# Scale of the first h summed on TensorE with its lower halves on VectorE, and the second layer's residual weighted beside the latent heads

## The chip, the cores and the metric

The kernel runs on one core of one Trainium2 chip. The metric is the device time of one launch in microseconds; of several runs the median is taken. The engines are named as in the profile: PE is TensorE (PEld its weight loads), DVE is VectorE, ACT is ScalarE, POOL is GpSimd, SP is SyncE, which here only issues DMAs.

## The reference

Two post-norm layers over x, 1024 tokens by 1024 features, batch 1, conditioned on one vector c:

```python
for l in range(DEPTH):
    mod = jax.nn.silu(c) @ w_ada[l] + b_ada[l]
    shift, scale, gate = jnp.split(mod, 3, axis=-1)
    h = x * (1.0 + scale[:, None, :]) + shift[:, None, :]
    (...) = jnp.split(h @ w_in[l], SPLIT_POINTS, axis=-1)
    ...  # o_a: 6 latent (MLA) heads, o_b: 6 dilated heads, o_c: 4 sparse heads with an indexer
    y = jnp.concatenate([o_a, o_b, o_c], axis=-1) * jax.nn.silu(p_gate)
    sub = y @ w_out[l]
    x = layer_norm(ALPHA * x + (1.0 + gate[:, None, :]) * sub, ln_g[l], ln_b[l])
```

Two things matter here. The first layer's `h` needs the scale and the shift, two products of a 1024-vector with a 1024x1024 matrix. And the second layer's residual is `ALPHA * x`, where x is the first layer's normalized output times `ln_g[0]` plus `ln_b[0]`.

## The kernel before, in words

**Precision.** A big fp32 product is made as three products of fp32r halves: an operand is split into a rounded upper half (`hi`, by ScalarE, AF.Copy) and a lower half (`lo = raw - hi`, by VectorE or GpSimd). `split_w` (L188) loads a weight tile into a raw buffer and makes both halves; its lower half is GpSimd's unless `lo_eng` says otherwise (L193).

**Order.** The program is written operation by operation; a scheduler with a timeline model (L1063) then sets the order of each engine's queue and inserts the waits, so the order of the code is a priority and not the order of execution. Each engine runs its own queue in order.

**The opening, `begin` (L883 to L946).** Eight steps, one for each block of 128 features. `part_ada(k)` loads two 128x1024 tiles of the modulation weights (e = 0 the scale, e = 1 the shift; w_ad0, L905). VectorE sums the tile's eight 128x128 pieces, weighted by the columns of silu(c) (`cs`): one operation at L913 and seven at L915. One fp32 matmul with a column of ones (L916) adds up the 128 partitions and leaves a column in the PSUM tile `o_ps` (O in the profile), and L918 adds the bias: `mod0`. `part_h(k)` loads x transposed (L922), in every other step a tile of the value weights `wvb` (L924, with a split), applies scale and shift on ScalarE (L927), rounds (L928), and makes the lower half at L929, on GpSimd but for the last step. `part_vb(k)` adds the step's 21 matmuls (three products for seven token blocks, L899) to seven PSUM banks. LEAD = 3 says how many steps `part_ada` is written ahead of `part_h`. The value blocks then leave PSUM (`values_b`), and the indexer follows (`indexer`, L387), whose first weights are split on GpSimd too, and beside which the other modulation vectors are summed on VectorE (`later`, `ada`, L256).

**The heads.** Each layer runs the dilated heads, the threshold search (`select`), the sparse heads and then the latent heads (`mla`, L679). In `attend` (L296) TensorE makes the scores of a block, VectorE takes the minimum on the way out of PSUM, ScalarE the exponential, GpSimd scales by the reciprocal of the sum (L293), TensorE transposes (L315), ScalarE and VectorE split (L318, L319), TensorE multiplies by the values (L327), and GpSimd applies the gate (L334). Other GpSimd work in `mla`: lower halves of keys (L721), of queries (L725) and of weights (L193).

**The end of a layer, `out_proj` (L792).** The gated y and the output weights are split (L800, L818). Then, for each block of 128 tokens in the order 7 to 0: the residual is loaded into a buffer of the ring XR (L841); two half rows of 24 matmuls each are multiplied by 1 + gate (L856), the residual is added (L857), statistics are taken (L858 to L863, with a power on GpSimd). In layer 1 the block is normalized and written to `x1_d` without ln_g and ln_b, which are folded into the next layer's scale and shift. In layer 2 the residual is therefore weighted first: GpSimd multiplies it by ln_g[0] (L843) and adds ln_b[0] (L844); the result is normalized with ln_g[1] and ln_b[1] at L867 and L868 and stored. XR has one buffer in layer 1 and two in layer 2. The four rows of ln_g and ln_b go to buffers that the heads have used (`lgb`, L824).

Of the kernel before, what the change touches and what calls it, by code (L numbers as in the profile page):

```python
# [13 lines left out]
OP = mybir.AluOpType  # L14
# [25 lines left out]

NLD = 8
NX = 6
LEAD = 3

NQ = ((2,2,3,4,6,6,6),(2,2,3,4,6,6,6))

# [14 lines left out]
KE = (1,1)  # L61

NPL = 2

EARLY = (2,2)
FB = ((0,2,4,0,2,0),(1,3,1,1,1,1))
# [40 lines left out]
def trunk(ctx: ExitStack, tc: tile.TileContext, a, out):  # L107
# [31 lines left out]
    scr, scr8 = [scrf[:, i * 256:i * 256 + 256].bitcast(mybir.dt.uint8) for i in range(2)]  # L139
    o_ps = ps_o.tile([P, 2, 256], F32, name="O")  # L140

    ident = sb.tile([P, P], F32, name="ident")
    causb = sb.tile([P, 512], BF16, name="causb")
    dist2 = sb.tile([P, 2 * P], BF16, name="dist2")
# [35 lines left out]
    kr_d = dr.tile([32, 1024], F32, name="kr_d")  # L180
    g1_d = [dr.tile([1, 1024], F32, name=f"g1_d{i}") for i in range(DEPTH)]
    x1_d = [dr.tile([P, 1024], F32, name=f"x1_d{i}") for i in range(NB)]


    def bc(t):
# [493 lines left out]
    def mla(l, values):  # L679
# [77 lines left out]

            project(wh, wl, 6, CA, evac)

        q, y = {}, {}  # L760
        keys(0)
        key(0)
        query(0)
# [4 lines left out]
        for h in range(6):  # L768
            if h % 2 == 0:
                y[h // 2] = G.next()  # L770
                sp.dma_start(y[h // 2], ga_d[h // 2])
            Kh, Kl = KA[h % 2]
            Qh, Ql = q[h]

            def done(g, yt=y[h // 2], yo=HA[h // 2], c=None):
                c = c or slice(g * 256, g * 256 + 256)
                act.activation(yo[0][:, c], yt[:, c], AF.Copy)
                pool.tensor_tensor(yo[1][:, c], yt[:, c], bc(yo[0][:, c]), OP.subtract)

            attend(f'A{h}', [(Qh, Kh), (Ql, Kh), (Qh, Kl)], vblk((h + 4) % 6), None, scq, y[h // 2],  # L780
                   (h % 2) * 64, ORDA[l], done if h in (3, 5) else None, PACK[l] and slots(h))
            if h < 4:
                if h % 2 == 0:
                    keys(h // 2 + 1)
                    if h == 2:
                        done(0, y[0], HA[0], slice(0, 1024))
                key(h + 2)
            for i in range(NQ[l][h], NQ[l][h + 1]):
                if i < 5:
                    query(i)  # L790

    def out_proj(l):  # L792
        last = l == DEPTH - 1
        order = [3, 4, 5, 6, 7, 0, 1, 2]
        Y = HA
        for k in order[:5]:
            raw = WR.next()
            sp.dma_start(raw, y_d[k])
            act.activation(Y[k][0], raw, AF.Copy)
            (pool if k in YP[l] else dve).tensor_tensor(Y[k][1], raw, bc(Y[k][0]), OP.subtract)  # L800


        Vs = [VS[0][:, i * 1024:(i + 1) * 1024] for i in range(6)]
        f = G.n % 2 ^ 1
        XR = Ring([AC[0]] + ([G.tiles[f]] if last else []))
        at = {3: (Vs[4], Vs[5]), 4: (Vs[0], Vs[1]), 5: W.tiles[0:2], 6: W.tiles[2:4],
              7: (fresh(f"g{1 - f}", F32R), fresh("bi1", F32R)), 0: held[0:2], 1: held[2:4],
              2: (Vs[2], [fresh(f"rw{n}", F32R, 512) for n in range(2)])}
        wo = {}
        for k in order:  # L810
            raw = WR.next()
            sp.dma_start(raw, a["w_out"][l, k])
            hi, lo = at[k]
            eng = pool if k in WP[l] else dve
            for n in range(2):
                c = slice(n * 512, n * 512 + 512)
                act.activation(hi[:, c], raw[:, c], AF.Copy)
                eng.tensor_tensor(lo[n] if k == 2 else lo[:, c], raw[:, c], bc(hi[:, c]), OP.subtract)  # L818
            wo[k] = [(hi[:, n * 512:n * 512 + 512], lo[n] if k == 2 else lo[:, n * 512:n * 512 + 512]) for n in range(2)]
        g1 = BI.tiles[0]  # L820
        sp.dma_start(g1, g1_d[l].to_broadcast([P, 1024]))
        lgb = []
        if last:
            for t, src in zip([fresh("pt0", F32), fresh("pt1", F32), PR3[2], PR3[1]],  # L824
                              (a["ln_g"][0], a["ln_b"][0], a["ln_g"][1], a["ln_b"][1])):
                sp.dma_start(t, src.to_broadcast([P, 1024]))
                lgb.append(t)
        else:

            lnc = small.tile([P, 2, 8], F32, name="lnc", bufs=1)  # L830
            sp.dma_start(lnc, a["ln_c"])
            dve.tensor_tensor(lnc[:, 0, :], lnc[:, 0, :], scale1_n, OP.mult)
            dve.tensor_tensor(lnc[:, 1, :], lnc[:, 1, :], scale1_n, OP.mult)
            dve.tensor_tensor(lnc[:, 1, :], lnc[:, 1, :], shift_n, OP.add)
        X = Ring(AC[1:4] + [PR3[0]])
        PR.tiles = [G.tiles[f]]
        xs = {}
        for tb in TBO:
            tok = slice(tb * P, (tb + 1) * P)
            xr = XR.next()  # L840
            sp.dma_start(xr, x1_d[tb] if last else a["x"][tb])  # L841
            if last:
                pool.tensor_tensor(xr, xr, lgb[0], OP.mult)  # L843
                pool.tensor_tensor(xr, xr, lgb[1], OP.add)  # L844
            r = X.next()
            st = small.tile([P, 2, 6], F32, name="st")
            for n in range(2):
                cols = slice(n * 512, n * 512 + 512)
                ps = (ps_p if n else ps_s).tile([P, 512], F32, name="pj" if n else "S")
                items = []  # L850
                for k in order:
                    yh, yl = Y[k]
                    w0, w1 = wo[k][n]
                    items += [(yh[:, tok], w0), (yl[:, tok], w0), (yh[:, tok], w1)]
                chain(ps, items)
                dve.tensor_tensor(r[:, cols], ps, g1[:, cols], OP.mult)  # L856
                dve.scalar_tensor_tensor(r[:, cols], xr[:, cols], ALPHA, r[:, cols], OP.mult, OP.add)  # L857
                dve.bn_stats(st[:, n, :], r[:, cols])  # L858
            mv = small.tile([P, 2], F32, name="mv")
            dve.bn_aggr(mv, st)  # L860
            rs = small.tile([P, 1], F32, name="rs")
            dve.tensor_scalar(rs, mv[:, 1:2], 1e-5, None, OP.add)  # L862
            pool.tensor_tensor(rs, rs, mhalf, OP.pow)  # L863
            if last:
                for n in range(2):
                    cols = slice(n * 512, (n + 1) * 512)
                    dve.scalar_tensor_tensor(r[:, cols], r[:, cols], mv[:, 0:1], lgb[2][:, cols], OP.subtract, OP.mult)  # L867
                    dve.scalar_tensor_tensor(r[:, cols], r[:, cols], rs, lgb[3][:, cols], OP.mult, OP.add)  # L868
                    sp.dma_start(out[tb][:, cols], r[:, cols])
                continue  # L870
            dve.tensor_scalar(r, r, mv[:, 0:1], rs, OP.subtract, OP.mult)
            sp.dma_start(x1_d[tb], r)
            xs[tb] = r
            if len(xs) == 4:
                for k in range(8):
                    t = ps_t.tile([P, 512], F32, name="T")
                    for j in range(4):
                        pe.transpose(t[:, j * P:(j + 1) * P], xs[tb // 4 * 4 + j][:, k * P:(k + 1) * P], ident)
                    mod_h(t, tb // 4, k, PR.next(), lnc[:, 0, :], lnc[:, 1, :])
                xs = {}  # L880


    def begin():  # L883
# [18 lines left out]
        def part_ada(k):  # L902
            for e in range(2):
                w = ring.next()
                sp.dma_start(w, a["w_ad0"][e, k])  # L905
                if k == 0 and e:
                    sp.dma_start(bcol, a["b_ad0"])
                    dve.tensor_scalar(bcol[:, 0, :], bcol[:, 0, :], 1.0, None, OP.add)
                part = cols[:, (2 * k + e) % 8, :]
                for c in range(8):  # L910
                    wc = w[:, c * P:(c + 1) * P]
                    if c == 0:
                        dve.tensor_scalar(part, wc, cs[:, 0:1], None, OP.mult)  # L913
                    else:
                        dve.scalar_tensor_tensor(part, wc, cs[:, c:c + 1], part, OP.mult, OP.add)  # L915
                pe.matmul(o_ps[:, 0, 2 * k + e:2 * k + e + 1], lhsT=part, rhs=ones, start=True, stop=True,  # L916
                          skip_group_check=True)
            dve.tensor_tensor(mod0[:, :, k], o_ps[:, 0, 2 * k:2 * k + 2], bcol[:, :, k], OP.add)  # L918

        def part_h(k):  # L920
            x = xs.next()
            sp.dma_start(x, a["xt"][k])  # L922
            if k % 2 == 0:
                hi, lo = split_w(a["wvb"][0, k // 2], 784, ring=QK, raws=raws)  # L924
                for j in range(2):
                    wv.append((hi[:, j * 392:(j + 1) * 392], lo[:, j * 392:(j + 1) * 392]))
            act.activation(x, x, AF.Identity, scale=mod0[:, 0, k:k + 1], bias=mod0[:, 1, k:k + 1])  # L927
            act.activation(HA[k][0], x, AF.Copy)  # L928
            (dve if k == 7 else pool).tensor_tensor(HA[k][1], x, bc(HA[k][0]), OP.subtract)  # L929

        for k in range(-LEAD, 9):
            if 0 <= k + LEAD < 8:
                part_ada(k + LEAD)
            if 0 <= k < 8:
                part_h(k)
            if k > 0:
                part_vb(k - 1)
        sp.dma_start(ident, a["ident"])
# [128 lines left out]
```

## Time and profile before

| | us |
|---|---|
| median of three runs | 1795.9 |
| the three runs | 1790.45 to 1797.68 |
| the profiled execution | 1791.37 |
| its span | 1789.5 |
| TensorE busy | 1662.4 |
| VectorE busy | 1396.6 |
| ScalarE busy | 1022.0 |
| GpSimd busy | 697.8 |

The span runs from the first instruction to the last; the remaining 1.9 us lie around it. A timeline row gives the start, the duration, the engine, the line, the operation, what it writes and reads, and how many were merged into the row; in brackets stands how long the engine was idle before it and what released it. In the rows of one line, three durations in ns are the shortest, the median and the longest. A row of the waits gives who waited for whom: us in total, times, and the longest. A row of the groups gives busy us, mean ns and the idle time before them.

### The profile page before, as it was taken

To read this page: it belongs to the slowest core of one execution; us is meant where nothing else is said; L and a number is where in the kernel's file an instruction comes from. 1 tells how busy PE (TensorE), PEld (TensorE's weight loads), DVE (VectorE), ACT (ScalarE), POOL (GpSimd) and SP (SyncE) were. 2 spreads that over 40 slices of the span, in tenths; PEclk is the share of its full clock that TensorE was granted. 3 is DMA by queue.
4 is the path that set the end of the run, shared out by engine and by line. 5 is a ranking of instruction groups with operands and counts; after the bars stand their busy time and mean duration, and the time that the engine had idled before them with its cause. 6 is when DMAs were issued, how large, how long until landed. Compare 5 with 4: busy or idle time off the path is not lost. (4 is left out here: it accounts for less than half of the span.)

```text
span 1789.5 us, 26735 instructions
## 1 busy us (share of the span) xinstructions
PE 1662.4 (93%) x9080; PEld 1440.0 (80%) x9080; DVE 1396.6 (78%) x3266; ACT 1022.0 (57%) x2010; POOL 697.8 (39%) x625
## 2 busy tenths in 40 slices
PE   4899899999998999989999989999999999998993
PEld 4778688888896888877899978888789788987882
DVE  8889788889588678886763678888948866788589
ACT  3244499895544666674113649998544367767500
POOL 3421134233434355463322113323343345666274
PEclk9899999999999999999999999999999999999997
DMA  9465113233212521222332212242220244122232
GB/s 345 147 220 189 48 55 92 78 119 102 75 36 62 212 92 57 84 68 92 110 130 51 71 59 56 75 142 83 74 92 20 67 171 141 45 76 91 71 106 94
DMA packets 55364, 178.93 MB, mean 100 GB/s; under 512 B 7606, under 2 KB 8630, under 8 KB 54716
## 3 DMA queue, kind: packets, MB, share of 16 engines
q1 hardware_dynamic: 50812, 147.86, 24.7%
q0 software_dynamic: 4416, 29.36, 5.7%
q8 instruction: 72, 1.18, 0.3%
q14 instruction: 64, 0.52, 0.1%
HBM read 129.74 MB, written 34.87 MB: 92 GB/s over the span
## 5 line engine op out<-in xcount | busy, mean ns | idle before, releaser
L199 PE MATMUL pj<-h,w 128*128 128x512 f32 (+1 forms) x3408 | 831.1, 391 | 13.9 <-DVE qk L233 5.4
L199 PEld LDWEIGHTS pj<-h,w 128*128 128x128 f32 x3408 | 632.2, 191 | 131.6 <-issue 12.6
L193 POOL TENSOR_TENSOR w<-wr,w 128x1024 fp32r<-128x1024 f32 (+2 forms) x86 | 192.9, 2244 | 284.4 <-ACT w L192 262.7
L199 PE MATMUL S<-qk,qk 128*128 128x512 f32 (+2 forms) x1104 | 281.9, 360 | 11.0 <-DVE mx L283 4.6
L293 POOL TENSOR_SCALAR pr<-pr,den 128x896 f32<-128x896 f32 (+7 forms) x180 | 139.0, 776 | 257.3 <-DVE den L292 214.0
L318 ACT ACTIVATE pt<-T 128x512 fp32r<-128x512 f32 (+1 forms) x320 | 172.1, 551 | 112.6 <-PE T L315 56.3
L319 DVE TENSOR_TENSOR pt<-T,pt 128x512 fp32r<-128x512 f32 (+1 forms) x320 | 199.6, 633 | 43.1 <-ACT pt L318 38.9
L327 PE MATMUL O<-pt,v 128*128 128x256 f32 (+1 forms) x1280 | 213.0, 286 | 7.3 <-DVE pt L319 4.2
L199 PEld LDWEIGHTS S<-qk,qk 128*128 128x128 f32 x1104 | 185.2, 191 | 36.7 <-DVE mx L283 8.7
L480 ACT ACTIVATE scr<-acc,U 128x768 uint8<-128x768 f32 x186 | 193.2, 1039 | 33.6 <-DVE U L476 18.1
L327 PEld LDWEIGHTS O<-pt,v 128*128 128x128 f32 x1280 | 185.6, 191 | 24.0 <-DVE pt L319 6.8
L334 POOL TENSOR_TENSOR g<-g,osum 64x256 f32<-64x256 f32 x128 | 98.6, 770 | 224.0 <-DVE osum L332 222.3
L291 ACT ACTIVATE pr<-pr,mx 128x384 f32<-128x384 f32 (+7 forms) x188 | 145.6, 775 | 54.7 <-DVE mx L283 36.4
L315 PE MATMUL T<-ident,pr 128*128 128x128 f32 x852 | 144.7, 278 | 9.7 <-POOL pr L293 5.1
L462 DVE TENSOR_SCALAR_CACHE_REDUCE scr<-acc,U 128x384 uint8<-128x384 f32 x186 | 138.4, 744 | 3.8
L192 ACT ACTIVATE w<-wr 128x1024 fp32r<-128x1024 f32 (+2 forms) x86 | 83.8, 976 | 65.0 <-PE pj L199 62.3
L315 PEld LDWEIGHTS T<-ident,pr 128*128 128x128 f32 x852 | 101.4, 141 | 21.0 <-POOL pr L293 6.5
L199 PE MATMUL pj<-w,h 128*128 128x256 f32 (+2 forms) x672 | 107.0, 300 | 1.4 <-DMA h<-cq_d 1.2
L199 PEld LDWEIGHTS pj<-w,h 128*128 128x128 f32 x672 | 91.7, 190 | 6.3 <-DMA h<-cq_d 1.4
L331 ACT ACTIVATE osum<-O 64x256 f32<-64x256 f32 x128 | 48.6, 380 | 58.5 <-PE O L327 55.3
L436 DVE SCALAR_TENSOR_TENSOR acc<-S,wi,acc 128x512 f32<-128x512 f32 (+1 forms) x84 | 56.2, 679 | 30.6 <-ACT S L431 30.3
L332 DVE TENSOR_TENSOR osum<-O,osum 64x256 f32<-64x256 f32 x128 | 53.4, 417 | 26.2 <-ACT osum L331 22.6
(277 smaller groups left out, 2565.2 us busy)
## 6 DMA issues: line engine op xcount, KB each, us to landing
wr<-in_wt_dram SPq DMA_DIRECT2D x62, 512.0 KB, 3.6
cq_d<-rw SPq DMA_DIRECT2D x64, 256.0 KB, 2.0
h<-cq_d POOLq DMA_DIRECT2D x4, 4096.0 KB, 20.2
qk<-qk POOLq DMA_DIRECT2D x48, 256.0 KB, 2.9
pt<-in_w_ada_dram SPq DMA_DIRECT2D x22, 512.0 KB, 4.0
wr<-in_w_out_dram SPq DMA_DIRECT2D x16, 512.0 KB, 3.5
bi<-in_bias_dram SPq DMA_DIRECT2D x14, 512.0 KB, 4.1
bi<-in_w_ada_dram SPq DMA_DIRECT2D x10, 512.0 KB, 4.5
```

The lines of the kernel that those rows point to most:

```text
L192: act.activation(hi[:, :n], raw[:, :n], AF.Copy)
L193: (lo_eng or pool).tensor_tensor(lo[:, :n], raw[:, :n], bc(hi[:, :n]), OP.subtract)
L199: pe.matmul(ps, lhsT=l, rhs=r, start=(i == 0), stop=(i == len(items) - 1))
L291: act.activation(p[:, :n], p[:, :n], AF.Exp, bias=m, scale=-1.0, accum_out=den)
L293: (dve if ne[qb] else pool).tensor_scalar(p[:, :n], p[:, :n], den, 0.5, OP.mult, OP.mult)
L315: pe.transpose(t[:, c:c + P], p[j](2 * kp + kk), ident)
L318: act.activation(pt[:, 0, :n], t[:, :n], AF.Copy)
L319: dve.tensor_tensor(pt[:, 1, :n], t[:, :n], bc(pt[:, 0, :n]), OP.subtract)
L327: pe.matmul(o[:, oc], lhsT=vt(kb), rhs=pt[:, e, pc], start=(kb == 0 and e == 0), stop=(kb == 2 * g + 1 and e == 1), skip_group_check=True)
L334: pool.tensor_tensor(yc, yc, s[r0:r0 + 64], OP.mult)
L462: dve.tensor_scalar(scr8[:, :IDX_LEN[b]], scores(b), s, None, op, OP.add, accum_out=dst[:, b:b + 1])
L480: act.activation(scr[:, :IDX_LEN[b]], scores(b), AF.Sign, bias=U[:, b:b + 1].bitcast(F32), accum_out=cnt[:, b:b + 1])
```

## The change

Three parts. First, in the opening, the scale half of the modulation (e = 0) is no longer summed on VectorE: eight fp32 matmuls per step take the 128x128 pieces of the raw weight tile as the stationary operand and a column of `cs` as the moving one, and accumulate in the same column of O. The shift half stays. The lower halves of h (L929) and of the value weights (`split_w` in `part_h`) go from GpSimd to VectorE. LEAD becomes 1, and `part_h(k)` is written ahead of `part_ada(k + 1)`.

Second, in layer 2 the weighted residual is made earlier: `residual(i)` loads a block of `x1_d` into a new tile RES, GpSimd multiplies by ln_g[0] and adds ln_b[0] (in the new tiles LNG and LNB), and the block is stored to `xw_d`. Two blocks are written after each of the heads 0 to 3 (NRES). `out_proj` of layer 2 loads `xw_d`; LNG and LNB then take ln_g[1] and ln_b[1].

Third, RES is a further buffer of the ring XR in both layers, so two in layer 1 and three in layer 2. The three new tiles take 12 KiB per partition; the scratch of the GpSimd-issued DMAs is set to 4096.

```diff
-LEAD = 3
+LEAD = 1
+NRES = ((0,0,0,0,0,0),(2,2,2,2,0,0))
...
+    RES, LNG, LNB = [sb.tile([P, 1024], F32, name=n) for n in ("res", "lng", "lnb")]
...
+    xw_d = [dr.tile([P, 1024], F32, name=f"xw_d{i}") for i in range(NB)]
...
-        q, y = {}, {}
+        q, y, rest = {}, {}, list(range(NB))
...
+            for _ in range(NRES[l][h]):
+                residual(rest.pop(0))
+
+    def residual(i):
+
+        if i == 0:
+            sp.dma_start(LNG, a["ln_g"][0].to_broadcast([P, 1024]))
+            sp.dma_start(LNB, a["ln_b"][0].to_broadcast([P, 1024]))
+        tb = TBO[i]
+        sp.dma_start(RES, x1_d[tb])
+        pool.tensor_tensor(RES, RES, LNG, OP.mult)
+        pool.tensor_tensor(RES, RES, LNB, OP.add)
+        sp.dma_start(xw_d[tb], RES)
...
-        XR = Ring([AC[0]] + ([G.tiles[f]] if last else []))
+        XR = Ring([AC[0], RES] + ([G.tiles[f]] if last else []))
...
-        lgb = []
         if last:
-            for t, src in zip([fresh("pt0", F32), fresh("pt1", F32), PR3[2], PR3[1]],
-                              (a["ln_g"][0], a["ln_b"][0], a["ln_g"][1], a["ln_b"][1])):
-                sp.dma_start(t, src.to_broadcast([P, 1024]))
-                lgb.append(t)
+            sp.dma_start(LNG, a["ln_g"][l].to_broadcast([P, 1024]))
+            sp.dma_start(LNB, a["ln_b"][l].to_broadcast([P, 1024]))
...
-            sp.dma_start(xr, x1_d[tb] if last else a["x"][tb])
-            if last:
-                pool.tensor_tensor(xr, xr, lgb[0], OP.mult)
-                pool.tensor_tensor(xr, xr, lgb[1], OP.add)
+            sp.dma_start(xr, xw_d[tb] if last else a["x"][tb])
...
-                    dve.scalar_tensor_tensor(r[:, cols], r[:, cols], mv[:, 0:1], lgb[2][:, cols], OP.subtract, OP.mult)
-                    dve.scalar_tensor_tensor(r[:, cols], r[:, cols], rs, lgb[3][:, cols], OP.mult, OP.add)
+                    dve.scalar_tensor_tensor(r[:, cols], r[:, cols], mv[:, 0:1], LNG[:, cols], OP.subtract, OP.mult)
+                    dve.scalar_tensor_tensor(r[:, cols], r[:, cols], rs, LNB[:, cols], OP.mult, OP.add)
...
-                part = cols[:, (2 * k + e) % 8, :]
+                to = o_ps[:, 0, 2 * k + e:2 * k + e + 1]
+                if e == 0:
+
+                    for c in range(8):
+                        pe.matmul(to, lhsT=w[:, c * P:(c + 1) * P], rhs=cs[:, c:c + 1], start=(c == 0), stop=(c == 7),
+                                  skip_group_check=True)
+                    continue
+
+                part = cols[:, k % 8, :]
...
-                hi, lo = split_w(a["wvb"][0, k // 2], 784, ring=QK, raws=raws)
+                hi, lo = split_w(a["wvb"][0, k // 2], 784, ring=QK, lo_eng=dve, raws=raws)
...
-            (dve if k == 7 else pool).tensor_tensor(HA[k][1], x, bc(HA[k][0]), OP.subtract)
+            dve.tensor_tensor(HA[k][1], x, bc(HA[k][0]), OP.subtract)
 
         for k in range(-LEAD, 9):
+            if 0 <= k < 8:
+                part_h(k)
             if 0 <= k + LEAD < 8:
                 part_ada(k + LEAD)
-            if 0 <= k < 8:
-                part_h(k)
...
-    nc = bacc.Bacc("TRN2", target_bir_lowering=False, num_devices=1)
+    nc = bacc.Bacc("TRN2", target_bir_lowering=False, num_devices=1, dynamic_dma_scratch_size=4096)
```

More of the change, by code (lines that the diff above doesn't have):

```diff
@@ L915, in part_ada @@
                         dve.scalar_tensor_tensor(part, wc, cs[:, c:c + 1], part, OP.mult, OP.add)
-                pe.matmul(o_ps[:, 0, 2 * k + e:2 * k + e + 1], lhsT=part, rhs=ones, start=True, stop=True,
-                          skip_group_check=True)
+                pe.matmul(to, lhsT=part, rhs=ones, start=True, stop=True, skip_group_check=True)
             dve.tensor_tensor(mod0[:, :, k], o_ps[:, 0, 2 * k:2 * k + 2], bcol[:, :, k], OP.add)
```

## The prediction

> **What bounds the kernel now.** I read the busy time by stretch of the span first, then the waits and the timeline of the two stretches in which TensorE is not busy.
>
> ```profile
> 0.00:74.30 74.30, 42.43 (x200) 39.45 (x200) 63.46 (x156) 25.48 (x28) 33.43 (x17) 0.93 0.71 255
> 74.30:1480.00 1405.70, 1352.07 (x7355) 1169.11 (x7356) 1091.79 (x2604) 848.35 (x1677) 488.15 (x455) 0.99 0.30 95
> 1480.00:1600.00 120.00, 119.22 (x744) 106.64 (x743) 91.09 (x245) 84.04 (x173) 72.47 (x73) 1.00 0.23 70
> 1600.00:1620.00 20.00, 14.45 (x86) 13.08 (x84) 16.22 (x34) 14.68 (x27) 16.72 (x11) 0.91 0.42 138
> 1620.00:1715.00 95.00, 90.92 (x510) 76.50 (x511) 63.46 (x144) 49.47 (x108) 45.10 (x51) 0.98 0.25 81
> 1715.00:1760.60 45.60, 43.34 (x190) 35.22 (x189) 45.46 (x50) 0.00 (x0) 32.94 (x15) 1.00 0.29 98
> 1760.60:1789.50 28.90, 0.00 (x1) 0.00 (x0) 25.16 (x39) 0.00 (x0) 8.96 (x6) 0.57 0.27 100
> ```
>
> Columns: the stretch, its length, busy time of PE, PEld, DVE, ACT, POOL, granted clock, DMA share, GB/s. From 74 to 1715 us TensorE is busy for 96% of the time: a change of another engine's work can bring little there. It idles in two places, 32 of the first 74 us and all of the last 29. The change touches both.
>
> The opening: a wait, and the timeline behind it.
>
> ```profile
> ACT v L927 <- DVE mod L918: 26.1, 4, 8.4
> ```
> ```profile
> 5.59 0.28 DVE L913 TENSOR_SCALAR g<-acc,cs 128x128 f32<-128x128 f32 x1 [2.64 <-DMA acc<-in_w_ad_dram]
> ```
> ```profile
> 24.36 2.44 POOL L929 TENSOR_TENSOR h<-v,h 128x1024 fp32r<-128x1024 f32 x1 [1.18 <-ACT h L928]
> 24.44 0.33 SPq L938 DMA_DIRECT2D ident<-in_ident_dram  x1
> 24.50 2.45 DVE L915 SCALAR_TENSOR_TENSOR g<-pr,cs,g 128x128 f32<-128x128 f32 x1
> ```
> ```profile
> 28.64 0.86 DVE L915 SCALAR_TENSOR_TENSOR g<-pr,cs,g 128x128 f32<-128x128 f32 x3
> ```
> ```profile
> 69.06 0.54 PEld L899 LDWEIGHTS S<-qk,h 128*128 128x128 f32 x3
> ...
> 73.67 0.34 PE L899 MATMUL T<-qk,h 128*128 128x392 f32 x1
> ```
>
> ScalarE waits 26.1 us, in four places, for the modulation (`mod0`, L918), which waits for VectorE's weighted sums: 128 operations (L913, L915). One L915 costs 0.86/3 = 0.29 us when three run in a row: 37 us in all. But VectorE is busy for 63 of the first 74 us. The rest is waiting that shows as busy time: an L915, both of whose inputs lie in SBUF, that starts beside a GpSimd subtraction of 2.44 us (L929) lasts 2.45 us. TensorE's own work there is 168 matmuls (L899) at 0.54/3 = 0.18 us, 30 us; the last ends at 74.0.
>
> The tail has the same picture, by engine:
>
> ```profile
> 1754.87 1.66 PE L199 MATMUL pj<-v,h 128*128 128x512 f32 x6 [2.26 <-DVE acc L856]
> 1756.36 1.52 PE L199 MATMUL pj<-w,h 128*128 128x512 f32 x6
> ...
> 1760.21 0.39 PE L199 MATMUL pj<-rw,h 128*128 128x512 f32 x1
> ```
> ```profile
> 1755.11 2.56 POOL L843 TENSOR_TENSOR acc<-acc,pt 128x1024 f32<-128x1024 f32 x1 [2.34 <-DMA acc<-x_d]
> 1757.75 2.72 POOL L844 TENSOR_TENSOR acc<-acc,pt 128x1024 f32<-128x1024 f32 x1
> ```
> ```profile
> 1755.45 5.58 DVE L868 SCALAR_TENSOR_TENSOR pr<-pr,rs,pr 128x512 f32<-128x512 f32 x2
> ...
> 1780.72 0.69 DVE L856 TENSOR_TENSOR pr<-pj,bi 128x512 f32<-128x512 f32 x1
> ...
> 1784.53 1.41 DVE L868 SCALAR_TENSOR_TENSOR pr<-pr,rs,pr 128x512 f32<-128x512 f32 x2
> ```
>
> Two L868 last 5.58 us beside L843 and L844, and 1.41 us where GpSimd is done with these. VectorE falls behind, holds TensorE for 2.26 us once, and has 25 us of work left when the last matmul ends at 1760.6.
>
> **The opening, after.** Removed from VectorE: the weighted sums of the scale, 64 operations, 64 x 0.29 = 18 us, and the contention, since L929 and the four value-weight splits leave GpSimd. Added to TensorE: 64 fp32 matmuls of one column. Added to VectorE: eight subtractions of 128x1024 and four of 128x784.
>
> ```profile
> 150.36 1.99 PEld L261 LDWEIGHTS O<-ones,g 128*128 128x128 f32 x16
> ```
> ```profile
> 9.40 0.50 PEld L916 LDWEIGHTS O<-ones,g 128*128 128x128 f32 x2 [9.40 <-DVE g L915]
> ```
> ```profile
> 39.29 1.24 ACT L927 ACTIVATE v<-v,mod 128x1024 f32<-128x1024 f32 x1 [4.54 <-DVE mod L918]
> 40.57 1.06 ACT L928 ACTIVATE h<-v 128x1024 fp32r<-128x1024 f32 x1
> ```
> ```profile
> L800 DVE TENSOR_TENSOR h<-wr,h x6: 1222/1762/2455, 743.3 to 1616.6; 128x1024 fp32r<-128x1024 f32 x6
> ```
> ```profile
> 5.60:23.40 17.80, 2.37 (x9) 2.02 (x9) 17.69 (x57) 4.46 (x5) 4.19 (x2) 1.00 1.00 395
> ```
>
> The same form of matmul (L261) loads its weights twice; eight of them take 1.99 us, 0.25 us each. TensorE gets 64 x 0.25 = 16 us and keeps the eight of the shift (2 us): 30 + 16 + 2 = 48. VectorE's load is 64 x 0.29 + 8 x 1.22 (L800 at its shortest, the same form) + 4 x 0.93 = 32 us. The transfers, 24 of 0.52 MB (scale, shift, x) and 4 of 0.40 (value weights), 14.2 MB, take 36 us at the 395 GB/s of 5.6 to 23.4 us. So TensorE bounds this stage next. It can start at 5.6. The first modulated x is there at 5.6 + 1.3 (the second weight tile, 0.52 MB) + 2.3 (eight sums) + 0.4 (matmul, add) + 2.3 (L927, L928) = 11.9; TensorE has 2 to 4 us of work until then and loses some 3: 5.6 + 48 + 3 = 57, 17 us before 74.0. I take **14**, for hand-overs: TensorE and VectorE write and read the one tile O in turn.
>
> Bounds: with no loss it ends at 54, a gain of 20. If the engines kept the order of the code, LEAD at 1 would make each step a loop of L927, L928, the subtraction, eight sums, matmul and add: 1.24 + 1.06 + 1.22 + 2.3 + 0.4 = 6.2 and half a us of hand-overs, seven times after 9.6, and then the last step's activations, subtraction and 21 matmuls, 7.3 us: 64, a gain of 10. They don't keep it: the load of `ident` (L938), written after the loop, is issued at 24.44, while the loop's last matmul runs at 73.67. So I expect the sums to run ahead of the subtraction. The upper price of a matmul is that of the row at 9.40, 0.50 us: 64 of these, 32 us, would leave a gain near 0. I take 0.25, since these too run eight in a row.
>
> The Trainium skill ("TensorE: Matmul & The Clock Gate", Part 1) says that TensorE runs at half its clock until it has been busy for about 3.4 us. By that rule some 16 of the new matmuls would be at the price of 9.40, 4 us more, and the gain 10; the trace agrees so far as a weight load at 9.40 takes 0.25 us and one at 69.06 0.18.
>
> What follows the opening starts earlier, and since TensorE is busy for 96% of it I count the gain in full.
>
> **The tail, after.** L843 and L844 leave it, 16 operations. Then no VectorE operation of two SBUF inputs waits there: a block costs two each of L856, L857, L858, L867 and L868 at 0.69 to 0.71 us and some 0.4 of small ones, 7.4 us, and TensorE needs 48 matmuls at (1.52 - 0.39)/5 = 0.226 us for it, 10.9. VectorE then keeps up, and TensorE ends 2.26 us earlier, at 1758.3. The last half block takes 5.2 us (1780.72 to 1785.94), and 3.5 us to the end of the span stand behind it. With 0.4 for the hand-over: 1767.4, a gain of **22**, and no more can be had, since TensorE's work is unchanged. The residual is now one load of `xw_d` in the same queue, with three buffers for two; where such loads come late, as in layer 1 with its single buffer (next row, L857's wait), some 7 of the 22 would stay: 15 is the lower bound.
>
> ```profile
>   DMA acc<-in_x_dram: 2.5, 3
> ```
>
> Layer 1's second buffer (RES) takes 0 to 2.5 us of these waits away; I take **1**.
>
> **The latent heads of layer 2, after.** They get 16 GpSimd operations of 128x1024, eight loads and eight stores, and two loads for the weights, during heads 0 to 4, about 1480 to 1620.
>
> ```profile
> L721 POOL TENSOR_TENSOR qk<-bi,qk 64x1024 fp32r<-64x1024 f32 x6 | 14.3, 2388 | 2.6 <-ACT qk L720 2.3 <-POOL pr L293 0.3
> ```
> ```profile
> L319 DVE TENSOR_TENSOR pt<-T,pt x320: 528/681/695, 244.9 to 1699.8; 128x512 fp32r<-128x512 f32 x96, 128x384 fp32r<-128x384 f32 x64
> ```
> ```profile
> DMA to landing us min/median/max: 2.6/2.8/3.6
> ```
>
> One takes 2.4 us (L721 has the same free size, 2.39): 38 us in all. GpSimd is idle for 47.5 us of 1480 to 1600 and 3.3 of 1600 to 1620. It stands on TensorE's path: it scales the probabilities (L293) before they are transposed, and behind a new operation an L293 waits up to 2.4 us. Yet the stage already holds six operations of this length (L721), and TensorE idles for 0.8 us in 120. Bounds: 0, and 38 if each reaches TensorE in full. I take **6**, near the lower end, most of it after 1600, where GpSimd is at 84% and TensorE already at 72%. VectorE's main work there reads PSUM (L319), and its longest case of 320 is 0.695 us: GpSimd doesn't hold it.
>
> The Trainium skill ("SBUF — State Buffer", Who interferes with whom) says that a VectorE operation with two SBUF inputs waits for a GpSimd one that reads SBUF, and one with a single SBUF input doesn't. By it only the weight splits (L800, L818) would wait beside the moved work; were it false for PSUM readers, up to 38 us of such waiting would move with it.
>
> **The sum** against the profiled execution's 1791.4 us (span 1789.5): -14 - 22 - 1 + 6 = -31, 1760.4. The median of the three runs is 4.5 above that execution; I add half of it: **1762.5**.
>
> **Rivals.** *The heads take it back:* GpSimd's queue delays L293 by half of the 38 us or more on TensorE's path; against it speaks the 0.8 us above. 1791 - 37 + 19 to 32: 1773 to 1786.
>
> *The opening doesn't shorten* (cold matmuls, or sums that come late over the one tile O): only the tail is won, with up to 4 us of the opening: 1791 - 22 - 1 + 6 less 0 to 4, 1770 to 1774.
>
> *Slower:* RES is one tile, so the residuals go in series: load 2.8, two operations 4.8, store 2.8, some 10.4 us each, 83 for eight. If a multiplication stands in GpSimd's queue while its load is on the way, all behind it (L293, L334, L725) waits too. GpSimd's idle 50 us can cover a part; from 46 us that reach TensorE (37 gained, 9 for 0.5%) the kernel is slower, and at two thirds of the 83 it takes 1791 - 37 + 55 = 1809. Against it: the loads need nothing of this layer and can be issued far ahead, as `ident` was.
>
> *The DMA scratch* (4096, while the new tiles take 12 KiB) makes GpSimd hold the second of the two big loads of a layer until the first has landed.
>
> ```profile
> q0 software_dynamic: 4416, 29.36, 5.7%
> ...
> h<-cq_d POOLq DMA_DIRECT2D x4, 4096.0 KB, 20.2
> ```
>
> That costs up to 20.2 us a layer, 40 in all: 1801. Against it: 4416 packets in 52 issues, over 16 DMA engines, are about 5 for an issue and an engine. The Trainium skill ("Debugging Trainium Hangs", 4. Descriptor Overflow) names 16 KiB per partition as room that too many descriptors overflow; no run here shows how much this kernel needs.
>
> **Chances.** The forecast (1747 to 1772) 0.60; the heads take it back 0.17; only the tail 0.11; slower 0.05; the scratch 0.02; better than the forecast 0.05 (1791 - 20 - 22 - 2.5 = 1746 with the heads free). The range leaves out the slower ones and the worst of the second: 1745 to 1785. A measurement can tell about 0.5%, 9 us, from no change. Faster by more: 0.60 + 0.05 + 0.11 + 0.10 of the 0.17, 0.86; within 0.07; slower 0.07.
>
> **What would show it.** Right: the opening's L899 end between 54 and 62 us, the new matmuls show about 0.25 us each, and ScalarE no longer waits 26 us for `mod`; in the tail L857 and L868 stay under 0.8 us and the span ends some 9 us after the last matmul; in the heads TensorE's idle time grows by no more than 10 us. Wrong: transposes that wait for L293 and L293 for the new operations; an L915 that still lasts over 2 us; a tail in which VectorE waits for loads of `xw_d`.

## The result, and the profile after

| | before | after |
|---|---|---|
| median | 1796.69 us (1790.45 to 1797.68, 4 runs) | 1751.24 us (1749.29 to 1755.10, 4 runs) |
| profiled execution, its span | 1791.37, 1789.5 us | 1750.43, 1748.6 us |
| ratio after to before | | 0.9757, 95% interval 0.9728 to 0.9785 |

The change is 2.4% faster: inside the predicted range, 11 us below the predicted time. In the code after, the lines up to the projections stand 5 further down (L199 is now L204), the output projection's 12 or 13 (L856 is L868, L857 L869, L868 L880), the opening's 12 to 20 (L899 is L911, L915 L935, L929 L948). The new lines are L925 (the matmuls of the scale) and L805 to L808 (the residual).

The page of the profile after, its busy times and the chain that ended last, by engine:

```profile
PE 1673.0 (96%) x9192; PEld 1451.5 (83%) x9192; DVE 1350.5 (77%) x3213; ACT 1019.8 (58%) x2010; POOL 666.9 (38%) x614
...
PE 53%; DVE 8%; ACT 3%; issue 2%; DMA 1%; POOL 1%; DVEq 0%; ACTq 0%; POOLq 0%
```

The busy time by stretch of the span after, with the columns of the prediction's first fence:

```profile
0.00:60.00 60.00, 52.25 (x305) 51.85 (x306) 40.07 (x99) 25.35 (x24) 5.10 (x6) 0.97 0.89 336
...
1460.00:1580.00 120.00, 119.21 (x756) 107.15 (x757) 91.22 (x245) 83.22 (x173) 69.10 (x72) 1.00 0.27 88
1580.00:1600.00 20.00, 16.53 (x105) 14.69 (x103) 16.86 (x39) 16.13 (x28) 19.33 (x12) 1.00 0.44 140
...
1690.00:1740.00 50.00, 50.00 (x222) 41.20 (x220) 41.08 (x75) 0.42 (x1) 8.02 (x9) 1.00 0.38 126
1740.00:1748.60 8.60, 0.15 (x1) 0.00 (x0) 5.09 (x9) 0.00 (x0) 0.92 (x1) 0.65 0.16 61
```

Both idle places have shrunk. In the opening TensorE is busy for 52 of 60 us, GpSimd for 5. In the last 50 us before its last matmul TensorE never idles, and 8.6 us stand behind that matmul, where there were 28.9. The latent heads' rows (1460 to 1600) are as they were: nothing was added there. The next fences show why: first the residual's rows by line, then those of the tail.

```profile
L806 POOL TENSOR_TENSOR res<-res,lng x8: 2369/2396/2404, 903.0 to 985.9; 128x1024 f32<-128x1024 f32 x8
its engine sat idle before it (us, times) until:
  DMA res<-x_d: 25.2, 8
```
```profile
L880 DVE SCALAR_TENSOR_TENSOR acc<-acc,rs,lnb x12: 699/744/747, 1693.3 to 1733.8; 128x512 f32<-128x512 f32 x12
```
```profile
DVE acc L868 <- PE pj L204: 4.0, 2, 3.3
```

The builder placed the eight weightings at the start of layer 2 (903 to 986 us), not beside the heads where the code has them. In the tail L880 (L868 of before) never lasts over 0.75 us, where the longest was 2.90, and in its last 60 us VectorE waits for TensorE (last row: us in total, times, longest), not the other way round.

For the experiments I cut each span at first and last starts by line: **opening** up to the last L911 (L899); **projection 1** from the first L868 (L856) to the last store of x1 (L884, L872); **indexer 2** from there to the last masked score (L446, L441); **tail** from the last load of a `y` tile (L776, L771) to the last L868. For after: 61.2; 829.1 to 902.0; to 1056.9; 1591.5 to 1740.2.

| us | ratio to before (95%) | opening | projection 1 | indexer 2 | tail | span |
|---|---|---|---|---|---|---|
| before | 1 | 73.7 | 75.3 | 151.0 | 172.9 | 1789.5 |
| after | 0.9757 (0.9728, 0.9785) | 61.2 | 72.9 | 154.9 | 148.7 | 1748.6 |
| open_only | 0.9945 (0.9928, 0.9961) | 61.5 | 75.5 | 151.3 | 173.2 | 1781.0 |
| scale_on_pe | 0.9976 (0.9963, 0.9989) | 70.8 | 75.2 | 151.1 | 173.4 | 1789.8 |
| low_on_dve | 0.9936 (0.9916, 0.9956) | 65.1 | 75.3 | 151.0 | 172.8 | 1778.0 |
| res_only | 0.9834 (0.9814, 0.9854) | 77.4 | 72.9 | 154.4 | 150.0 | 1760.9 |
| low_res | 0.9767 (0.9744, 0.9790) | 64.3 | 72.9 | 154.4 | 148.3 | 1748.9 |
| six_on_pe | 0.9816 (0.9793, 0.9838) | 69.6 | 72.9 | 155.3 | 150.0 | 1760.9 |
| pool_beside_tail | 0.9859 (0.9842, 0.9876) | 61.5 | 72.8 | 155.0 | 168.0 | 1768.4 |
| res_in_heads | 0.9833 (0.9814, 0.9852) | 63.3 | 72.9 | 152.9 | 165.1 | 1764.9 |
| xr_as_before | 0.9831 (0.9809, 0.9854) | 62.1 | 86.0 | 157.8 | 149.8 | 1764.5 |
| res_unused | 1.0069 (1.0042, 1.0096) | 74.1 | 83.7 | 157.2 | 171.7 | 1801.1 |
| layout_only | 0.9988 (0.9972, 1.0003) | 74.6 | 75.3 | 151.0 | 173.0 | 1794.4 |
| one_op | 1.0022 (1.0010, 1.0034) | 77.0 | 75.3 | 151.0 | 172.7 | 1793.2 |

### The profile page after: what moved, and what is told of

Same layout as the page of the kernel before. It is cut to its first block, busy times and chain, and to the rows that moved or that the text cites. A ratio compares the mean times of both kernels' runs of the same rounds, so it can differ in the third digit from the quotient of the medians.

```text
span 1748.6 us, 26930 instructions
## 1 busy us (share of the span) xinstructions
PE 1673.0 (96%) x9192; PEld 1451.5 (83%) x9192; DVE 1350.5 (77%) x3213; ACT 1019.8 (58%) x2010; POOL 666.9 (38%) x614
## 4 chain that ended last, share of the span: by engine, by line
PE 53%; DVE 8%; ACT 3%; issue 2%; DMA 1%; POOL 1%; DVEq 0%; ACTq 0%; POOLq 0%
PE pj L204 30%; PE S L204 12%; PE O L332 5%; PE T L320 5%; DVE pt L324 1%; ACT pt L323 1%; PE T L204 1%; ACT scr L485 1%; DVE acc L543 0%; DVE pr L536 0%; DVE acc L441 0%; PE T L890 0%; DVE h L818 0%; DVE acc L291 0%; ACT pr L296 0%
## 5 line engine op out<-in xcount | busy, mean ns | idle before, releaser
L204 PE MATMUL pj<-h,w 128*128 128x512 f32 (+1 forms) x3408 | 833.0, 391 | 13.9 <-DVE qk L238 5.8
L204 PEld LDWEIGHTS pj<-h,w 128*128 128x128 f32 x3408 | 629.9, 190 | 131.1 <-issue 11.9
L204 PE MATMUL S<-qk,qk 128*128 128x512 f32 (+2 forms) x1104 | 279.7, 358 | 8.4 <-DVE mx L288 3.1
L204 PEld LDWEIGHTS S<-qk,qk 128*128 128x128 f32 x1104 | 184.2, 190 | 33.4 <-DVE mx L288 6.4
L204 PE MATMUL pj<-w,h 128*128 128x256 f32 (+2 forms) x672 | 107.0, 300 | 0.2 <-ACT w L835 0.2
L204 PEld LDWEIGHTS pj<-w,h 128*128 128x128 f32 x672 | 91.7, 190 | 5.1 <-ACT w L835 0.5
L441 DVE SCALAR_TENSOR_TENSOR acc<-S,wi,acc 128x512 f32<-128x512 f32 (+1 forms) x84 | 55.7, 678 | 23.0 <-ACT S L436 22.8
```

What stands on the lines that cost most here:

```text
L204: pe.matmul(ps, lhsT=l, rhs=r, start=(i == 0), stop=(i == len(items) - 1))
```

## The experiments

The theory: both places lost their time to VectorE operations on SBUF that stretch beside GpSimd's. Its rivals: the instructions that left the path (the scale's sums, the two GpSimd operations between load and sum), the order that the builder lays, or the memory's layout.

**The opening's part alone, and each half of it.** open_only is before with the change's `part_ada`, `part_h`, loop and LEAD. The halves: scale_on_pe is open_only with the two edits below, low_on_dve is before with both of them the other way round.

```diff
-hi, lo = split_w(a["wvb"][0, k // 2], 784, ring=QK, lo_eng=dve, raws=raws)
+hi, lo = split_w(a["wvb"][0, k // 2], 784, ring=QK, raws=raws)
-dve.tensor_tensor(HA[k][1], x, bc(HA[k][0]), OP.subtract)
+(dve if k == 7 else pool).tensor_tensor(HA[k][1], x, bc(HA[k][0]), OP.subtract)
```

> The opening's part alone (scale on TensorE, lower halves on VectorE, LEAD 1, the new order); residual, XR and DMA scratch as before. Theory: the parts add up. The opening's 168 matmuls end at about 61 us instead of 74, some 15 us are won by the end of layer 1's indexer, and the tail keeps its 29 us after the last matmul: 1781 us, ratio 0.9915. Rival: the tail's gain needs the opening's shifted order too (the scheduler's order differs everywhere), then this kernel wins clearly more or less than 15.

> As open_only, but the lower halves of h and of the value weights stay on GpSimd (h's last block on VectorE), as before. Theory (waiting beside GpSimd counts as much as the number of operations): VectorE has 64 sums, 22 us, and some 25 us of waiting beside eleven GpSimd subtractions; that fits beside TensorE's 48 us only partly, the opening ends at 62 to 67 us and the kernel takes 1782 to 1787 us. Rival (only the number of VectorE's operations counts): as open_only, 1781.

> The lower halves of h and of the value weights on VectorE, and nothing else changed: the scale is still summed on VectorE, LEAD 3, the order as before. Theory (waiting counts): VectorE does 128 sums at 0.29 us and twelve subtractions, 51 us without waits, for the 59 it spends now on the sums alone; the opening ends some 6 to 9 us earlier, 1787 to 1790 us. Rival (only the number of operations counts): twelve more operations on the engine that bounds the stage, 0 to 14 us later, 1796 to 1810.

Measured: 1784.0, 1789.7 and 1780.9 us beside 1794.2. The weighted sums by line, in scale_on_pe and in low_on_dve (count, then ns least/median/most):

```profile
L923 DVE SCALAR_TENSOR_TENSOR g<-acc,cs,g x28: 350/352/2384, 6.7 to 57.2; 128x128 f32<-128x128 f32 x28
```
```profile
L915 DVE SCALAR_TENSOR_TENSOR g<-acc,cs,g x56: 331/340/352, 5.9 to 49.8; 128x128 f32<-128x128 f32 x56
```

With the lower halves still on GpSimd and half of the sums gone, some sums last 2.38 us. With all of the sums still there and the lower halves on VectorE none of these 56 lasts over 0.35, and of the other 56 the longest lasts 2.48, beside a weight split of the indexer, which GpSimd still has. VectorE got eleven operations more (the subtraction of h's last block was its own before) and the kernel became 13 us faster: here the waiting counts, not the work. Moving the scale without them brings 0.2%.

**The residual's part alone.** res_only is the change with the opening of before.

> The residual's part alone (weighting moved, RES in XR, DMA scratch 4096); the opening as before. Theory: 20 us from the end after the last matmul and 2 from TensorE's wait in the tail, less 2 us that the moved work costs at layer 2's start, where the trace of the changed kernel shows it: 1775 us, ratio 0.989. Rival: the 4 us that the changed kernel wins between head 4 of layer 2 and the last matmul also belong to this part: 1771, ratio 0.986.

Measured: 1763.6 us, 30.6 below before, more than either expectation. Its tail is 22.9 us shorter, projection 1 2.4, indexer 2 3.4 longer. Its opening, of which nothing was edited, ends 3.7 us later than that of before. The rest, some 10 us, is spread over other stages of which nothing was edited; two runs further down are about it.

**Both without the scale on TensorE.** low_res is res_only with the two edits of low_on_dve.

> The kernel before with the residual part and the lower halves on VectorE, the scale left on VectorE with three blocks of lead. Theory (the two parts add, and the scale on TensorE is worth little): 1763.6 less 13.3 is about 1750 us, as fast as the whole change, 1748 to 1753. Rival (the scale on TensorE is worth what the opening showed, about 4 us at its end): 1754 to 1757.

Measured: 1751.5 us, the time of the whole change. The opening ends 3 us earlier with the 64 matmuls and LEAD 1 (64.3 to 61.2), and the total shows none of it; the five kernels with the change's opening end it between 61.2 and 63.3, so these 3 us are hardly told from the order that the builder lays. The waits of low_res in its first 78 us say that TensorE has room there:

```profile
PEld O L928 <- DVE g L927: 21.1, 8, 9.4
```

**Fewer sums on TensorE.** six_on_pe takes two blocks of the scale back to VectorE, with the change's LEAD of 1.

```diff
-if e == 0:
+if e == 0 and k % 4 != 3:
...
-part = cols[:, k % 8, :]
+part = cols[:, (2 * k + e) % 8, :]
```

> The change with the scale of blocks 3 and 7 summed on VectorE again, so that TensorE sums six. Theory (TensorE bounds the change's opening, VectorE has room): the opening ends 2 to 4 us earlier than 61 us, the whole at 1748 to 1750. Rival (the later stages take it back, as they did between one part and the whole): within 2 us of 1751. If VectorE's chain is what ends the opening: 1753 to 1756.

Measured: 1762.1 us, slower than every expectation; the opening ends 8.4 us later than in the change. The wait of ScalarE for the modulation, here and in the change (us in total, times, longest):

```profile
ACT v L946 <- DVE mod L937: 25.0, 7, 6.4
```
```profile
ACT v L946 <- DVE mod L937: 13.1, 7, 2.8
```

It is 25.0 us for 13.1. With sums on VectorE only one step ahead (LEAD 1), two blocks of 16 sums hold up the activation behind them; low_res has all the sums on VectorE, three steps ahead, and loses nothing. So the scale on TensorE is worth something where LEAD is 1, and LEAD was not tried by itself.

**GpSimd at work beside the tail.** The change, with two operations per block back on GpSimd whose result nobody reads (`ta` and `tb_` are the unused tiles pt0 and pt1, `tb_` loaded):

```diff
 sp.dma_start(xr, xw_d[tb] if last else a["x"][tb])
+if last:
+    pool.tensor_tensor(ta, xr, tb_, OP.mult)
+    pool.tensor_tensor(ta, xr, tb_, OP.add)
```

> The change, with two more GpSimd operations of 128x1024 per row block in the tail that read xr and a loaded row and write a tile that nobody reads (sixteen operations of 2.4 us, about 38 us). Theory A (in the tail before, VectorE and GpSimd slowed each other or VectorE's evictions waited while GpSimd was at work): 1757 to 1770 us, VectorE's L868-type operations in the tail at above 1 us. Theory B (the tail lost its time to the two GpSimd operations on the path from load to sum, not to their presence): within 3 us of 1751.

Measured: 1769.1 us, 18 above the change, as theory A has it. Rows of its tail: GpSimd's new operation, VectorE's L885 and L873 (L880 and L868 of the change), and what TensorE waits for.

```profile
L885 DVE SCALAR_TENSOR_TENSOR acc<-acc,rs,lnb x12: 737/2512/2891, 1698.5 to 1757.4; 128x512 f32<-128x512 f32 x12
```
```profile
1734.52 4.92 DVE L885 SCALAR_TENSOR_TENSOR acc<-acc,rs,lnb 128x512 f32<-128x512 f32 x2
...
1736.21 2.68 POOL L861 TENSOR_TENSOR pt<-g,pt 128x1024 f32<-128x1024 f32 x1
...
1739.36 0.68 DVE L873 TENSOR_TENSOR acc<-pj,bi 128x512 f32<-128x512 f32 x1
...
1740.09 2.50 PE L204 MATMUL pj<-v,h 128*128 128x512 f32 x5 [3.30 <-DVE acc L873]
```

L885, two inputs in SBUF, rises from 0.74 to a median of 2.51 us in these twelve; TensorE then waits 3.30 us for an eviction (L873) that stood behind it. No VectorE operation needs the new operations' result, and the profile lists no wait of VectorE from 1690 to 1765 us, neither for a load nor for GpSimd's power. So of the tail's 24 us, 19 (168.0 against 148.7) come back by GpSimd's presence. The Trainium skill ("SBUF — State Buffer", Who interferes with whom) says that an operation with at most one input in SBUF, outside the two-port modes, is not held. That agrees with L873, which reads PSUM and one SBUF tile: it lasts 0.68 and 0.67 us where GpSimd is at work, as in the tail without it (0.68, L868 after).

```profile
1748.36 2.67 POOL L860 TENSOR_TENSOR pt<-res,pt 128x1024 f32<-128x1024 f32 x1
1748.76 0.68 DVE L873 TENSOR_TENSOR acc<-S,bi 128x512 f32<-128x512 f32 x1
...
1751.11 2.67 POOL L861 TENSOR_TENSOR pt<-res,pt 128x1024 f32<-128x1024 f32 x1
...
1752.22 0.67 DVE L873 TENSOR_TENSOR acc<-pj,bi 128x512 f32<-128x512 f32 x1
```

One input in SBUF is no guarantee by itself. In the opening of before, L913 reads one SBUF tile and writes another; its median is 0.28 us, and two of the sixteen, which started beside GpSimd's operations, lasted 1.89 and 2.48 us. The prediction gave the rule without that exception; in which mode these two ran no run shows.

```profile
L913 DVE TENSOR_SCALAR g<-acc,cs x8: 271/280/1894, 5.6 to 51.4; 128x128 f32<-128x128 f32 x8
L913 DVE TENSOR_SCALAR g<-bi,cs x4: 278/280/2483, 11.8 to 55.7; 128x128 f32<-128x128 f32 x4
```

**The residual where the code has it.** Nothing in the change ties the weightings to the heads. Here a one-column copy of a head's `y` tile into RES does.

```diff
+if NRES[l][h]:
+    rr = slice((h % 2) * 64, (h % 2) * 64 + 64)
+    dve.tensor_copy(RES[rr, 0:1], y[h // 2][rr, 256:257])
 for _ in range(NRES[l][h]):
     residual(rest.pop(0))
```

> The change, with a one-column copy per head from the y tile into RES, so that the weighting of the residual stands behind the latent heads 0 to 3 of layer 2 and cannot be placed ahead of them. Theory (the prediction's heads term): about 1757 us, that is 6 us above the change as it is, bounds 1751 to 1789; the GpSimd work between heads delays the next head's cast and row maxima. Rival (GpSimd has room there): within 2 us of 1751. If the pairs lose their GpSimd time serially: 1789.

Measured: 1763.8 us, 12.6 above the change. Its residual, the wait of SP's queue for it, and pieces of the chain that ended last:

```profile
L809 POOL TENSOR_TENSOR res<-res,lng x8: 2343/2396/2795, 1559.9 to 1677.9; 128x1024 f32<-128x1024 f32 x8
```
```profile
SPq L811 <- POOL res L810: 36.8, 7, 9.0
```
```profile
1609.16 6.15 DMA wr<-in_w_out_dram
1615.99 1.29 DVE v L839 x2
1617.31 3.68 DMA wr<-in_w_out_dram
```

Up to the last load of a `y` tile nothing is lost (1591.4 us, 1591.5 in the change). The tail behind it is 16.4 us longer (165.1 against 148.7). The rows hold two reasons. SP's queue stands 36.8 us in front of the stores of RES, and the loads of W_out, which share that queue, are on the chain. And the splits of y and of W_out on VectorE (L821 and L839, two inputs in SBUF) stretch beside the moved work: from 1580 us on they last 30.2 us, 20.0 in the change (L818 and L836). The splits of y in both layers, here and in the change:

```profile
L821 DVE TENSOR_TENSOR h<-wr,h x6: 1220/2363/4605, 731.2 to 1605.3; 128x1024 fp32r<-128x1024 f32 x6
```
```profile
L818 DVE TENSOR_TENSOR h<-wr,h x6: 1218/1826/2612, 728.2 to 1598.7; 128x1024 fp32r<-128x1024 f32 x6
```

How the 16 us divide is not shown; no run took the stores to another queue.

**The ring of residual buffers without RES.**

```diff
-XR = Ring([AC[0], RES] + ([G.tiles[f]] if last else []))
+XR = Ring([AC[0]] + ([G.tiles[f]] if last else []))
```

> The change without RES in the ring of residual buffers: layer 1's output projection has one buffer again, layer 2's two. Theory (the prediction's third term): 1 us slower than the change, 1752 us, bounds 0 to 2.5. Rival (two buffers are too few in the tail now that the blocks need no GpSimd, or one in layer 1 waits longer): 1754 to 1760.

Measured: 1764.3 us, 13 above the change, outside the theory and past the rival. The tail is 1.1 us longer; projection 1 takes 86.0 us instead of 72.9. Its rows: the residual's first start, the waits of L869 by what ended them, and the busy time of 828 to 915 us here and in the change.

```profile
L806 POOL TENSOR_TENSOR res<-res,lng x8: 2367/2390/2649, 846.8 to 944.0; 128x1024 f32<-128x1024 f32 x8
```
```profile
L869 DVE SCALAR_TENSOR_TENSOR pr<-acc,pr x4: 693/1564/2736, 850.0 to 907.3; 128x512 f32<-128x512 f32 x4
...
  DMA acc<-in_x_dram: 8.6, 5
```
```profile
828.00:915.00 87.00, 81.95 (x392) 69.63 (x390) 61.54 (x92) 13.05 (x22) 49.20 (x32) 0.98 0.53 185
```
```profile
828.00:915.00 87.00, 87.00 (x443) 75.70 (x442) 63.91 (x103) 15.61 (x27) 33.54 (x27) 1.00 0.40 146
```

With RES in the ring the first weighting has to wait until the projection of layer 1 has given RES back. Without it the weightings start at 846.8, inside that projection (828.7 to 914.7), and the loads of `x` come late and L869 is stretched, both of which the rows show and neither of which was tried alone. So RES in the ring is a buffer and, more than that, a lock.

**The weighted residual that nobody reads.** res_only with the tail, and the ring, of before.

> The residual part at the start of layer 2 as in the change, opening as before, but the tail of before: it weights the residual itself once more and the weighted blocks in DRAM are read by nobody. Theory (the tail's edits are worth about 22 us, the rest of the residual part's gain of 30 comes from elsewhere): 1764 plus 22, about 1786 us, ratio 0.995 to 0.997. Rival (all 30 us are the tail's): 1794 us or 1796 with the extra work, ratio 0.999 to 1.003.

Measured: 1806.5 us, slower than before. Tail 171.7, much as before; projection 1 83.7, since this kernel has no RES in its ring either; indexer 2 157.2. The expectation overlooked the lock, so the run can't price the tail's edits by its total. By stage it can: its tail is 171.7 us, and that of xr_as_before, with the same buffers in its ring but the weighting out of the tail, 149.8, so 22 us lie there. And it confirms another thing: the residual's part costs 8 us in projection 1 and 6 in indexer 2 where nothing holds it back.

**The layout, and a new order by itself.** layout_only is before with the DMA scratch of 4096 and the three tiles unused; one_op has that scratch and adds one load and one GpSimd operation on an unused tile at the end of the opening.

```diff
+RES, LNG, LNB = [sb.tile([P, 1024], F32, name=n) for n in ("res", "lng", "lnb")]
-nc = bacc.Bacc("TRN2", target_bir_lowering=False, num_devices=1)
+nc = bacc.Bacc("TRN2", target_bir_lowering=False, num_devices=1, dynamic_dma_scratch_size=4096)
```

> The kernel before with the change's DMA scratch of 4096 bytes and its three tiles RES, LNG and LNB allocated and left unused; every engine's order of instructions is that of the kernel before. Question: the residual part gains about 5 us ahead of the tail, most of it in layer 1's indexer stage, where nothing of it was edited. Theory (the order): the builder ordered the instructions anew, so here nothing changes: 1793 to 1796 us, ratio 0.9985 to 1.0015, layer 1's indexer stage 132 us as before. Rival (the memory's layout or the descriptors' ring): 1788 to 1790 us, ratio 0.996 to 0.998, with that stage at 127.5 to 129.5 us.

> The kernel before with one load of 128x1024 at the end of the opening and one GpSimd operation of some 2.4 us on it, into a tile that nobody reads, and the change's DMA scratch. The builder then orders the instructions otherwise (3213 of 9046 TensorE rows stand elsewhere) with the work all but equal. Theory (the order of the instructions that the builder lays anew is worth some us by itself): the time differs from the kernel before by 2 to 8 us either way, ratio 0.995 to 0.999 or 1.001 to 1.005, and layer 1's indexer stage by 2 us or more. Rival (the order is worth nothing): ratio 0.9985 to 1.0015, the stage 132 us.

Measured: 1790.3 us (0.9988) and 1797.0 us (1.0022). The layout is worth nothing that can be told from none. My question to it was wrong in part: with the instructions of before in the order of before, its profile shows layer 1's indexer, from the opening's end to the first masked score, at 135.8 us (74.6 to 210.4), where before's shows 132.6. So that stage is read from one profile to some 3 us. Yet the 4 to 5 us that I meant to explain are not all doubt: the stage lasts 128.3 to 131.4 us in all eight kernels that hold the residual's part, and 132.3 to 135.9 in all six that don't. The busy time of that stage in before and in the change:

```profile
73.70:206.30 132.60, 126.48 (x605) 106.82 (x604) 112.54 (x156) 60.64 (x122) 24.78 (x12) 0.97 0.54 175
```
```profile
61.20:190.80 129.60, 123.95 (x606) 105.21 (x605) 113.33 (x156) 59.82 (x121) 25.63 (x12) 0.99 0.56 180
```

The same matmuls keep TensorE busy for 2.5 us less, at a higher granted clock (0.99 for 0.97). Why the residual's part, which adds no work there, goes with that, no run shows; one_op has 0.99 too and stays at 132.3.

one_op's new order costs 0.2%; but layer 2's selection and query stages (from the last masked score to the last `h<-cq_d`) take 390.1 us in it, 393.7 in before and 391.7 in the change. So 2 to 4 us there come with a new order that has no useful edit.

## Why the prediction was right or wrong

**What bounds the kernel:** right. Of the 40.9 us between the two spans, 12.5 come from the opening and 24.5 from the tail and what ends it.

**The opening, 14:** 12.5 at its end, inside its bounds. The price of a matmul was right once TensorE is warm and not before; weight loads of the new matmuls (start, us for 16):

```profile
5.33 3.49 PEld L925 LDWEIGHTS O<-cs,acc 128*128 128x128 f32 x16 [5.33 <-issue]
...
11.36 3.49 PEld L925 LDWEIGHTS O<-cs,acc 128*128 128x128 f32 x16 [1.20 <-DVE mod L937]
...
25.75 1.93 PEld L925 LDWEIGHTS O<-cs,g 128*128 128x128 f32 x16
```

1.93/8 = 0.24 us a matmul, and 3.49/8 = 0.44 for the first sixteen: 3.1 us more. The rule that the prediction set beside its own price came out in size (some 16 matmuls, 4 us). In time it did not: the slow price outlasts the 3.4 us of busy time. TensorE is busy without a pause from 11.36 on, and three weight loads of L911 still take 0.98 us at 17.56, and 0.54 only at 19.38. And that it is half a clock is not shown: the granted clock reads 1.00 from 5 to 19 us. VectorE's operations came out as worked out but for the sums:

```profile
L948 DVE TENSOR_TENSOR h<-v,h x8: 1217/1225/1227, 13.7 to 55.9; 128x1024 fp32r<-128x1024 f32 x8
```
```profile
6.93 2.68 DVE L935 SCALAR_TENSOR_TENSOR g<-acc,cs,g 128x128 f32<-128x128 f32 x7
```

2.68/7 = 0.38 us, not 0.29. The reading that all of VectorE's 63 us but the 37 were waiting went too far: ten stretched sums of before account for some 19 of the 26 us, the rest is other work. What the step missed is which half matters: it put the 18 us of removed sums beside the contention as if they counted alike. The lower halves alone bring 8.6 of the 12.5 us at the opening's end (65.1), and with the residual's part the whole change's time.

**The tail, 22:** right in mechanism, 24.2 and 0.3 behind it by the spans. The predicted 9 us behind the last matmul are 8.5 (1740.1 to 1748.6). The loads of `xw_d` did not come late.

**Layer 1's second buffer, 1:** 2.4, in every kernel that has it (75.3 to 72.9). That it also locks the residual out of that projection was not seen at all: without RES in the ring it takes 86.0 us, 10.7 more than before's 75.3.

**The heads, +6: the step that failed.** It took the place in the code for the place in time. The prediction used that very argument in favour of the change for `ident`, whose load the builder had hoisted, and named it against the slower rival, but did not ask where the weightings themselves would go: they need only x1, and went to 903 us. There they cost 3.9 us of indexer 2 (151.0 to 154.9), a place with no term. Where they are forced beside the heads the price is 12.6, twice my 6 and within 0 to 38. The rows put it on SP's queue and on the stretched splits, which the prediction had named without a price, not on the L293 that I watched: TensorE waits 0.3 us for it there, as in the change.

**The sum.** Predicted -31, measured -40.9 between the spans. Opening +1.5, tail and end -2.5, buffer -1.4, heads -6.0, indexer 2 +3.9: -4.5. The other -5.4 have no term: layer 1's indexer -3.0, whose cause stays open, layer 2's selection and query stages -2.0, of the size that one_op shows without any useful edit, and small ones -0.4. So the range held in part by its width: of the 9.9 us by which the sum was off, over half have no term. And I added 2.1 us for the median, where 0.8 stood between the profiled execution and the median.

**The rivals:** the DMA scratch held no load up; the row after, where before has 20.2:

```profile
h<-cq_d POOLq DMA_DIRECT2D x4, 4096.0 KB, 19.1
```

The heads did take back 13 where they were made to; the slower rival's serial RES is seen in the 25.2 us for which GpSimd waits for its loads, at a place where little else needs GpSimd (it is busy for 25 of the 100 us from 900 on in before). That the opening doesn't shorten is ruled out by its 12.5 us.

## What to carry to other kernels

Before an engine's work is priced, look for the operations of another engine that stretch beside it: eleven operations more on VectorE made this kernel 13 us faster, because GpSimd's went. Ask of every moved piece what holds it where the code puts it; if nothing but its inputs does, the builder will place it by these, and a buffer shared with the stage ahead can be the lock that keeps it out. And before looking for the cause of a stage's few us, see how far that stage moves between kernels in which nothing of it was edited: here 0.3 us for layer 1's projection (75.2 to 75.5 in six kernels), 3.6 for its indexer (132.3 to 135.9 in the same six).

## What the runs showed of the hardware that was not expected

A sum that needs the one before it costs 0.38 us for 128x128 on VectorE (L935 after, 2.68 us for seven), while three in a row of before took 0.86, 0.29 each, where more than one tile's sums ran in turn. The trace of before bears that out: its own first three sums, which had only one tile to work on, also took 0.38 each.

```profile
5.91 1.13 DVE L915 SCALAR_TENSOR_TENSOR g<-acc,cs,g 128x128 f32<-128x128 f32 x3
```

A stretched VectorE operation ends just behind the GpSimd operation beside it, whatever its own length: in the prediction's rows L929 ends at 24.36 + 2.44 = 26.80 and L915 at 24.50 + 2.45 = 26.95, for 0.34 us of work; in the tail 0.74 us lasted 2.5.
